# A hybrid encoder block on one core: 27 instead of 24 pairs of the down projection by seven products, activation sums made during up, the value branch without its row norm, taps on ScalarE, weights laid out by the host

## The chip, the cores and the metric

One Trainium2 chip, one of its cores. The time is that of the whole program on the device, in microseconds, as the median of several executions. A second number is the span of one profiled execution, from its first to its last instruction; the profile's rows all come from that execution. TensorE multiplies matrices and writes to PSUM, VectorE and ScalarE do elementwise work on SBUF and PSUM, GpSimd (POOL) does a few tiny operations here, and SyncE (SP) issues nearly all transfers, in order.

## The reference

One layer over 256 tokens of width 2048, in float32. The parts that this change touches are the channel mixer and the way in which every weight is read:

```python
def conv_glu(hn, w_up, conv_w, conv_b, w_down):
    up = hn @ w_up                                   # 2048 -> 2 x 5632
    gate, val = jnp.split(up, 2, axis=-1)
    gate = dwconv_centred(gate, conv_w, conv_b)      # 3 taps along the tokens
    return (jax.nn.gelu(gate, approximate=True) * val) @ w_down

mix = jnp.concatenate([y_ssd, y_pool], axis=-1) @ w_out[i]
h = h + rmsnorm(mix, mix_norm_post[i])
hn = rmsnorm(h, ffn_norm_pre[i])
ff = conv_glu(hn, w_ffn_up[i], ffn_conv_w[i], ffn_conv_b[i], w_ffn_down[i])
h = h + rmsnorm(ff, ffn_norm_post[i])
gate = jax.nn.sigmoid(rmsnorm(h, ple_norm_pre[i]) @ w_ple_gate[i])
h = h + rmsnorm(gate * (p[i] @ w_ple[i]), ple_norm_post[i])
```

In front of it stand an input projection (`w_in`: z, xbc, and dt with u), a state-space mixer and a pooling mixer.

## The kernel before

**Precision.** Each float32 operand is split into a high part (rounded to the form that TensorE takes at full rate) and a low part (the rest). A product of two split operands is three matmuls: high x high, high x low, low x high. `split` makes the parts of a piece of weights: a cast on ScalarE (L152) and a subtraction on VectorE (L153), into one of five pairs of buffers (`whi`, `wlo`). `raw` gives one of three 1 MB buffers that weights are loaded into, on SP's queue through `load` (L119).

**Stages**, in order: dtu (dt and u of the input projection), xbc in three slabs (`feature_major`), z (`token_major`) with the state-space work beside it, wo (the output projection, a `sublayer`), ple's first half, up, down (`dn`, a `sublayer`), ple's second half, the gate (`gt`).

**Up** runs 11 slabs of 512 features. In each, `feature_pairs` makes two pieces `ga` of 256 gate features and two pieces `va` of 256 values, each with tokens along the free side, in two loads of 1 MB; after each load it calls `aside`, which takes the next list of jobs from `work` (88 lists in up). `total` adds the two halves of a piece's PSUM result. The norm in front of up is put on afterwards: `rfb` holds the reciprocal norm of every token along the free side. The gate is multiplied by it (L882), goes through `conv` (centre tap with bias on ScalarE L422, the two others on VectorE L428), through gelu (L884), and is multiplied by `rfb` a second time (L885), which stands for the value's norm; the values are multiplied by that and land in `hid` (L895), six page buffers that stay for down. `rf`, one number per token along the partitions, is what `rfb` was made from.

**Seven products.** Down takes 44 blocks of 128 rows of `w_down`, two at a time: 22 pairs, for each of two halves of the 2048 output columns. An ordinary pair in `token_major` takes 2 blocks x 2 token halves x 2 column halves x 3 = 24 matmuls of 128 x 512. A pair named in `fast` goes through `seven_products`: it takes the pair as a 2 x 2 block product in seven block products instead of eight, 21 matmuls, from four sums of weight blocks (`add_blocks`) and four sums of activation blocks (`pair_sums`); `combine` puts the seven results together at the end of the half. The weight sums of down and of the gate are made during up by `block_sums`, as four jobs: `fetch` the pair, nothing, `add`, `store` to DRAM; the last two in the list are `held` in their page buffers. In down a fast pair then loads three quarters of its weights (`raw`) and its sums (`t`, a page buffer). The activation sums come from `hid_sums`, in a `mid` buffer (three of them): four small operations (L777 to L780) and a split (L781, L782). Those of four pairs (`dn_keep`) are kept in two page buffers from half 0 to half 1. `get_hid` (L903, L904) splits the activations of a pair.

**Around down.** `at` names things to do before a pair of half 1: `back` (before pair 13) loads h again, which was put in DRAM in front of up; `first_gate` (before pair 16) loads the first pair of the gate's weights, casts it twice on ScalarE (L948, L950) and adds into the low part by a transfer on POOL's queue (L949). After each half `sublayer` squares the results on ScalarE (L823) and multiplies them by the norm's gain on VectorE (L824); then h is updated (L831) and transposed for the gate (L380), with ple's second half between.

**Buffers.** 13 page buffers of 1 MB (`page`), three `mid` buffers of half that, PSUM with six `main` and two `misc` banks. The framework orders each engine's instructions before the run, by its own estimate of when each can start; on the chip each engine then runs its own in that order.

Of the kernel before, what the change touches and what calls it, by code (L numbers as in the profile page):

```python
# [16 lines left out]
P = 128  # L17
L = 256
# [33 lines left out]
def build(nc, a, out):  # L52
    x = a["x"][0]
    w_in, w_out, w_up = a["w_in"][0], a["w_out"][0], a["w_ffn_up"][0]
    w_down, w_gate, w_ple = a["w_ffn_down"][0], a["w_ple_gate"][0], a["w_ple"][0]
    out = out[0]

    with tile.TileContext(nc) as tc, \
# [37 lines left out]
        c_dt = DSSD + 1536  # L96
        r0 = wp.tile([P, 2048], F32, tag="raw", bufs=3, name="dtur0")
        for n in range(2):
            first = ins(nc.scalar.dma_start(r0[:, n * 352:(n + 1) * 352],
                                            w_in[:P, c_dt + n * 352:c_dt + (n + 1) * 352]))  # L100
# [55 lines left out]
        def raw(name, src, a_, b_):  # L156
            r = wp.tile([P, 2048], F32, tag="raw", bufs=3, name=name)
            if src is None:
                return r
            last["dma"] = load(r[:, :a_ * b_].rearrange("p (a b) -> p a b", a=a_), src, True)  # L160
            return r
# [46 lines left out]
        def block_sums(name, w, c0, k, held):  # L208
# [4 lines left out]
            def fetch():  # L213
                r = page(f"{name}b{c0}_{k}")
                pg.append(r)
                load(r.rearrange("p (k c) -> p k c", k=2),
                     w[k * P:(k + 2) * P, c0:c0 + 1024].rearrange("(k p) c -> p k c", p=P))
# [6 lines left out]
            def store():  # L224
                if not held:
                    t = dp.tile([P, 2048], F32, tag=f"{name}s{c0}_{k}", bufs=1, name=f"{name}s{c0}_{k}")
                    load(t, pg[0])
                    sums_[name, c0, k] = t, False

            return [fetch], [], [add], [store]  # L230

        def add_blocks(r):

            v = r.rearrange("p (b c) -> p b c", b=4)
            nc.vector.tensor_add(v[:, 0:2], v[:, 0:2], v[:, 1::2])  # L235
            nc.vector.tensor_add(v[:, 3], v[:, 3], v[:, 0])
            nc.vector.tensor_add(v[:, 2], v[:, 2], v[:, 3])

        def seven_products(name, stage, w, k0, c0, a_, acc, alt, start, stop):
# [3 lines left out]
            if (stage, c0, k0) in sums_:  # L243
                r = raw(f"{name}r", None, 0, 0)
                last["dma"] = load(r[:, 512:1536], w[(k0 + 1) * P:(k0 + 2) * P, c0:c0 + 1024], True)
                last["dma"] = load(r[:, :512], w[k0 * P:(k0 + 1) * P, c0:c0 + 512], True)
# [4 lines left out]
                b11 = split(f"{name}a", r[:, :512], 512)  # L251
                b2 = split(f"{name}b", r[:, 512:1536], 1024)
            else:
                r = t = raw(f"{name}r", w[k0 * P:(k0 + 2) * P, c0:c0 + 1024]
                            .rearrange("(k p) c -> p k c", p=P), 2, 1024)
                b11 = split(f"{name}a", r[:, :512], 512)
                b2 = split(f"{name}b", r[:, 1024:], 1024)
# [3 lines left out]
            for x, (wh, wl), c, o, own in (  # L261
                    ("a11", b11, 0, alt[0], True), ("a12", b2, 0, acc[0][0], False), ("s4", b2, 512, acc[0][1], False),
                    ("s1", t13, 0, alt[1], True), ("s3", t13, 512, alt[2], True), ("a22", t42, 0, acc[1][0], False),
                    ("s2", t42, 512, alt[3], True)):
# [26 lines left out]
        def token_major(name, w, c0, ks, get, acc, tail=1, fast=(), alt=None, sums=None, at=()):  # L291
# [3 lines left out]
            for u in range(nu):  # L295
# [3 lines left out]
                if u in fast:  # L299
                    if u == fast[0]:  # L300
# [3 lines left out]
                r = None if f"{name}{k0}_0" in ready else raw(f"{name}r{k0}", w[k0 * P:(k0 + 2) * P, c0:c0 + 1024]  # L304
                                                               .rearrange("(k p) c -> p k c", p=P), 2, 1024)
# [8 lines left out]
                for t, (o, c), (k, wh, wl), q in order:  # L314
                    xh, xl = (v[:, t * P:(t + 1) * P] for v in get(k))
                    xx, ww = ((xh, wh), (xh, wl), (xl, wh))[q]
                    mm(o, xx, ww[:, c:c + o.shape[-1]], k == ks[0] and q == 0, k == ks[-1] and q == 2)
# [3 lines left out]
                aside()  # L321

        def feature_major(name, w, c0, get, acc):

            for u in range(4):
                r = raw(f"{name}r{u}", w[u * 512:(u + 1) * 512, c0:c0 + 512]
                        .rearrange("(k p) c -> p k c", p=P), 4, 512)
# [12 lines left out]
        def feature_pairs(name, w, c0, get, acc):  # L340


            for u in range(2):
                r = raw(f"{name}r{u}", w[u * 1024:(u + 1) * 1024, c0:c0 + 256]
                        .rearrange("(k p) c -> p k c", p=P), 8, 256)
# [97 lines left out]
        for u in range(0, NK, 2):  # L443
            r = [wp.tile([P, 2048], F32, tag="raw", bufs=3, name=f"dtur{u}") if u else r0, page(f"dtur{u + 1}")]
            for j in range(2):
                k = u + j
                if k == 0:
                    last["dma"] = load(r[0][:, 704:1056], w_in[:P, c_dt + 704:c_dt + 1056])
# [3 lines left out]
                for c0, c1 in ((0, 704), (704, 1056)) if k == 1 else ((0, 1056),):  # L452
                    last["dma"] = load(r[j][:, c0:c1], w_in[k * P:(k + 1) * P, c_dt + c0:c_dt + c1])
# [29 lines left out]
        with tc.issue_after(half[0]), tc.issue_after(half[1]):  # L483
# [11 lines left out]
            for a_ in range(4):  # L495
# [17 lines left out]
        load(pmat.rearrange("p (g s t) -> p g s t", g=4, s=2),  # L513
             a["pool_matrix"].rearrange("g (s p) t -> p g s t", p=P))
        poolw = page("poolw")
        load(poolw.rearrange("p (g c d) -> p g c d", g=4, c=2),
             a["pool_w"][0].rearrange("g (c p) d -> p g c d", p=P))
# [122 lines left out]
        def xbc(slab):  # L640
            acc = main(f"xbc{slab}")
            feature_major(f"xb{slab}", w_in, DSSD + slab * 512, hn, acc)
# [88 lines left out]
        token_major("z", w_in, 0, list(range(NK)), hn, zacc)  # L731
# [43 lines left out]

# [144 lines left out]
        def hid_sums(k):  # L920
# [3 lines left out]
            if k not in kept:  # L924
# [6 lines left out]
                if n >= 0:  # L931
                    kept[k] = d
# [157 lines left out]
```

## Time and profile before

| | us |
|---|---|
| median of three runs | 1122.8 (1122.64 to 1123.46) |
| the profiled execution | 1123.46 |
| its span | 1121.6 |

The chain of work that ended last, by what it ran on (share of the span), gives the stages their weight:

```profile
PE va L87 22%; PE ga L87 21%; PE dna L87 14%; PE woa L87 7%; PE xbc L87 6%; PE gt L87 5%; PE z L87 4%; PE dtu L87 4%; PE dns L87 3%; PE dn0s L87 1%; PE dn1s L87 1%; PE ple L87 1%; PE pw L87 1%; PE yd L87 1%; DMA dtur<-w_in 0%
```

`va` and `ga` are up, `dna` the accumulators of down, `dns`, `dn0s` and `dn1s` its four further ones for the seven products. Line 87 is the helper `mm` that issues every matmul, so groups are told apart by tile and not by line. PE is TensorE, PEld its weight loads, DVE VectorE, ACT ScalarE.

Transfers, by queue (packets, megabytes, share of the time of 16 DMA engines), and four of the issues (size, median time from issue to landing):

```profile
q1 hardware_dynamic: 145216, 298.19, 78.8%
q0 software_dynamic: 272, 1.05, 0.5%
...
dnb<-w_ffn_down SPq DMA_DIRECT2D x24, 1024.0 KB, 10.3
dns<-dnb SPq DMA_DIRECT2D x22, 1024.0 KB, 6.9
dn0r<-w_ffn_down SPq DMA_DIRECT2D x10, 1024.0 KB, 6.2
dn1r<-w_ffn_down SPq DMA_DIRECT2D x10, 1024.0 KB, 6.9
```

q1 is SP's queue, q0 POOL's. `dnb` is the fetch of a pair for its weight sums, `dns` their way to DRAM.

### The profile page before, as it was taken

Reading aid. Unit: us, or ns where it says so; the run is one execution under the profiler, and the core shown is the slowest. Engines: PE = TensorE matmul, PEld = TensorE weight load, DVE = VectorE, ACT = ScalarE, POOL = GpSimd, SP = SyncE. Lnnn points to the kernel's source line nnn. Section 1 sums busy time; section 2 is a strip of 40 time slices with the busy share of each in tenths; the row PEclk is TensorE's granted clock in tenths of the full one; section 3 lists DMA queues with packets and bytes.
Section 4 is the critical chain, followed back from the end, with each engine's and each line's share of the span. In section 5 each row is a group of like instructions: output and inputs, shape, how many; then the busy total and the mean of one; then the engine's idle time right before and its main releaser. Section 6 shows DMA issues by size and latency. Waiting matters only on the chain.

```text
span 1121.6 us, 15747 instructions
## 1 busy us (share of the span) xinstructions
PE 1111.2 (99%) x5975; PEld 957.1 (85%) x5975; DVE 928.0 (83%) x1291; ACT 665.4 (59%) x929; POOL 31.1 (3%) x69
## 2 busy tenths in 40 slices
PE   9999999999999999999999999999999999999997
PEld 9999988888888888888888888888888888888876
DVE  6468897799898877877877768878799999899795
ACT  6848663555764554554545545545677777786673
POOL 0200000100100000000000000000000000001001
PEclk9999999999999999999999999999999999999999
DMA  9853447456799989999999898996969688995673
GB/s 361 312 197 104 162 161 277 151 188 189 252 320 349 316 298 340 303 295 313 341 319 310 289 335 303 313 297 218 321 198 336 219 292 295 381 323 175 231 235 107
DMA packets 145996, 300.87 MB, mean 268 GB/s; under 512 B 5504, under 2 KB 98560, under 8 KB 137856
## 3 DMA queue, kind: packets, MB, share of 16 engines
q1 hardware_dynamic: 145216, 298.19, 78.8%
q0 software_dynamic: 272, 1.05, 0.5%
q8 instruction: 47, 0.77, 0.3%
q10 hardware_dynamic: 432, 0.62, 0.2%
q14 instruction: 29, 0.24, 0.1%
HBM read 268.38 MB, written 31.46 MB: 267 GB/s over the span
## 4 chain that ended last, share of the span: by engine, by line
PE 95%; ACT 2%; DVE 1%; issue 1%; DMA 0%; POOL 0%; SPq 0%; POOLq 0%; ACTq 0%
PE va L87 22%; PE ga L87 21%; PE dna L87 14%; PE woa L87 7%; PE xbc L87 6%; PE gt L87 5%; PE z L87 4%; PE dtu L87 4%; PE dns L87 3%; PE dn0s L87 1%; PE dn1s L87 1%; PE ple L87 1%; PE pw L87 1%; PE yd L87 1%; DMA dtur<-w_in 0%
## 5 line engine op out<-in xcount | busy, mean ns | idle before, releaser
L87 PE MATMUL ga<-wox,ug_0h 128*128 128x512 f32 x352 | 125.5, 395 | 0.0
L87 PE MATMUL ga<-wox,ug_1h 128*128 128x512 f32 x352 | 125.1, 394 | 0.0
L87 PE MATMUL va<-wox,uv_1h 128*128 128x512 f32 x352 | 124.8, 393 | 0.0
L87 PE MATMUL va<-wox,uv_0h 128*128 128x512 f32 x352 | 124.8, 393 | 0.0
L87 PE MATMUL ga<-wox,ug_1l 128*128 128x256 f32 x352 | 99.2, 282 | 0.0
L87 PE MATMUL ga<-wox,ug_0l 128*128 128x256 f32 x352 | 99.1, 282 | 0.0
L87 PE MATMUL va<-wox,uv_1l 128*128 128x256 f32 x352 | 99.1, 281 | 0.0
L87 PE MATMUL va<-wox,uv_0l 128*128 128x256 f32 x352 | 99.1, 281 | 0.0
L87 PEld LDWEIGHTS va<-wox,uv_1h 128*128 128x128 f32 x352 | 66.1, 188 | 15.0
L87 PEld LDWEIGHTS va<-wox,uv_0h 128*128 128x128 f32 x352 | 66.1, 188 | 15.0
L87 PEld LDWEIGHTS ga<-wox,ug_0h 128*128 128x128 f32 x352 | 66.1, 188 | 14.9
L87 PEld LDWEIGHTS ga<-wox,ug_1h 128*128 128x128 f32 x352 | 66.1, 188 | 14.9
L87 PEld LDWEIGHTS ga<-wox,ug_0l 128*128 128x128 f32 x352 | 66.2, 188 | 0.1
L87 PEld LDWEIGHTS ga<-wox,ug_1l 128*128 128x128 f32 x352 | 66.2, 188 | 0.0
L87 PEld LDWEIGHTS va<-wox,uv_1l 128*128 128x128 f32 x352 | 66.2, 188 | 0.0
L87 PEld LDWEIGHTS va<-wox,uv_0l 128*128 128x128 f32 x352 | 66.2, 188 | 0.0
L87 PE MATMUL dna<-dn_0h,hs 128*128 128x512 f32 x160 | 50.1, 393 | 0.0
L87 PE MATMUL dna<-dn_1h,hs 128*128 128x512 f32 x160 | 49.9, 393 | 0.0
L235 DVE TENSOR_TENSOR dnb<-dnb 128x1024 f32<-128x1024 f32 x24 | 29.3, 1222 | 14.0 <-DMA dnb<-w_ffn_down 14.0
L903 ACT CAST hs<-hid 128x512 fp32r<-128x512 f32 x44 | 27.1, 617 | 18.3 <-PE dna L87 18.3
L904 DVE TENSOR_TENSOR hs<-hid,hs 128x512 fp32r<-128x512 f32 x44 | 30.2, 686 | 9.1 <-ACT hs L903 9.0
L428 DVE SCALAR_TENSOR_TENSOR fc<-gr,vt,fc 128x255 f32<-128x255 f32 x88 | 36.8, 479 | 0.1
(1909 smaller groups left out, 3060.3 us busy)
## 6 DMA issues: line engine op xcount, KB each, us to landing
dnb<-w_ffn_down SPq DMA_DIRECT2D x24, 1024.0 KB, 10.3
dns<-dnb SPq DMA_DIRECT2D x22, 1024.0 KB, 6.9
dn0r<-w_ffn_down SPq DMA_DIRECT2D x10, 1024.0 KB, 6.2
dn1r<-w_ffn_down SPq DMA_DIRECT2D x10, 1024.0 KB, 6.9
zr<-w_in SPq DMA_DIRECT2D x8, 1024.0 KB, 5.2
dtur<-w_in SPq DMA_DIRECT2D x14, 528.0 KB, 8.5
wo0r<-w_out SPq DMA_DIRECT2D x7, 1024.0 KB, 5.5
wo1r<-w_out SPq DMA_DIRECT2D x6, 1024.0 KB, 5.7
```

The costliest lines, as they stand in the source:

```text
L87: last["pe"] = ins(nc.tensor.matmul(o, lhsT, rhs, start=start, stop=stop, skip_group_check=True))
L235: nc.vector.tensor_add(v[:, 0:2], v[:, 0:2], v[:, 1::2])
L428: nc.vector.scalar_tensor_tensor(o[:, lo:hi], i[:, lo + d:hi + d], vec(wcol + j * wstep + f), o[:, lo:hi], op0=ALU.mult, op1=ALU.add)
L903: nc.scalar.copy(t[:, :512], src)
L904: nc.vector.tensor_sub(t[:, 512:], src, t[:, :512].bitcast(F32))
```

## The change

1. **More fast pairs.** Half 0 of down takes 14 of its 22 pairs by seven products and half 1 takes 13, for 12 and 12. `block_sums` makes 27 + 4 sets of sums for 24 + 4, at 14/5 slots of `work` apart instead of 3; the two held ones have no fourth slot.
2. **Activation sums from up.** For eight pairs (`dn_stored`, fast in both halves) the sums of activations are made during up, in an `hs` buffer, and stored to DRAM; in down `hid_sums` loads them on POOL's queue into a `mid` buffer, in both halves. For the other fast pairs they are made in down, in each half. The kept page buffers go.
3. **Values without the norm.** The second multiplication by `rfb` goes. The token's factor is put on in `sublayer` instead (`row=rf`): as a scale of the squares and in a three-operand multiply with the gain.
4. **Taps on ScalarE.** `conv` of up is written out per half slab: three taps on ScalarE into `cv`, `tp` and the source itself, added by two VectorE adds over two features at once; gelu per half slab.
5. **Weights in tiles by the host.** Every weight comes as tiles of 128 rows x 2048 (1056 for dtu), in the order in which they are read, so that one load reads one stretch of memory. In `pairs` the first block of a pair has its column halves swapped, so that the three quarters that a fast pair needs lie together: one load in place of two. The pooling constants are laid out the same way.
6. **Order.** `add_blocks` takes four instructions of 512 columns for one of 1024 and two of 512. The seven products come in another order, with the split of the second half of the sums first. `first_gate` (now `first`) stands before pair 15 instead of 16, `back` behind the last pair instead of before pair 13.

```diff
             def store():
-                if not held:
-                    t = dp.tile([P, 2048], F32, tag=f"{name}s{c0}_{k}", bufs=1, name=f"{name}s{c0}_{k}")
...
-            return [fetch], [], [add], [store]
+            return [[fetch], [], [add]] + [[store]] * (not held)
 
         def add_blocks(r):
             v = r.rearrange("p (b c) -> p b c", b=4)
-            nc.vector.tensor_add(v[:, 0:2], v[:, 0:2], v[:, 1::2])
-            nc.vector.tensor_add(v[:, 3], v[:, 3], v[:, 0])
-            nc.vector.tensor_add(v[:, 2], v[:, 2], v[:, 3])
+            for i, j in ((1, 0), (0, 3), (3, 1), (2, 3)):
+                nc.vector.tensor_add(v[:, i], v[:, i], v[:, j])
...
             if (stage, c0, k0) in sums_:
-                r = raw(f"{name}r", None, 0, 0)
-                last["dma"] = load(r[:, 512:1536], w[(k0 + 1) * P:(k0 + 2) * P, c0:c0 + 1024], True)
-                last["dma"] = load(r[:, :512], w[k0 * P:(k0 + 1) * P, c0:c0 + 512], True)
+                r = raw(f"{name}r")
+                last["dma"] = load(r[:, 512:], w[c0 // 1024, k0 // 2][:, 512:], True)
...
-            t13 = split(f"{name}c", t[:, :1024], 1024)
             t42 = split(f"{name}d", t[:, 1024:], 1024)
+            t31 = split(f"{name}c", t[:, :1024], 1024)
...
-                        nc.scalar.activation(junk, b, AF.Square, accum_out=q)
-                        nc.vector.tensor_mul(mg[t][:, c], b, gain[:, c])
+                        if row:
+                            nc.scalar.activation(junk, b, AF.Square, scale=row[t], accum_out=q)
+                            nc.vector.scalar_tensor_tensor(mg[t][:, c], b, row[t], gain[:, c], op0=ALU.mult, op1=ALU.mult)
...
-        dn_fast, gt_fast, dn_keep = ((2, 3, 5, 7, 8, 10, 12, 13, 15, 16, 18, 19), (2, 3, 5, 7, 8, 10, 12, 13, 15, 16, 18, 19)), ((4, 6), (1, 2)), (3, 8, 13, 18)
+        dn_fast, gt_fast = ((2, 3, 4, 5, 7, 8, 9, 11, 12, 13, 15, 16, 18, 19), (2, 3, 5, 7, 8, 9, 11, 12, 13, 15, 16, 18, 19)), ((4, 6), (1, 2))
+
+        dn_stored = (2, 3, 5, 8, 11, 13, 16, 19)
...
-                work[3 * i + 2 + j].extend(jobs)
+                work[14 * i // 5 + 1 + j].extend(jobs)
...
+        def hid_sums_jobs(k):
+            o = []
+            def make():
+                o.append(lp.tile([P, 1024], F32R, tag="hs", bufs=2, name=f"he{k}"))
+                hid_sums_of(k, o[0][:, 512:].bitcast(F32), o[0])
+            def store():
+                kept[k] = dp.tile([P, 1024], F32, tag=f"hsum{k}", bufs=1, name=f"hsum{k}")
+                load(kept[k], o[0].bitcast(F32))
+            return [make], [store]
+        for u in dn_stored:
+            for j, jobs in enumerate(hid_sums_jobs(2 * u)):
+                work[u // 2 * 8 + u % 2 * 2 + 6 + j].extend(jobs)
...
-            cv = conv(f"fc{s}", sc, 3, V_FCW + 4 * s, NF, V_FCB + 4 * s)
-            nc.scalar.activation(cv, cv, AF.Gelu_apprx_tanh)
-            nc.vector.tensor_tensor(cv.rearrange("p (f t) -> p f t", f=4), cv.rearrange("p (f t) -> p f t", f=4),
-                                    rfb.unsqueeze(1).to_broadcast([P, 4, L]), op=ALU.mult)
+                c, l = (m[:, i * 512:(i + 1) * 512].rearrange("p (f t) -> p f t", f=2) for m in (cv, tp))
+                for f in range(2):
+                    w = V_FCW + 4 * s + 2 * i + f
+                    nc.scalar.activation(c[:, f], v[:, f], AF.Identity, bias=vec(V_FCB + 4 * s + 2 * i + f), scale=vec(w + NF))
+                    nc.scalar.activation(l[:, f], v[:, f], AF.Copy, scale=vec(w))
+                    nc.scalar.activation(v[:, f], v[:, f], AF.Copy, scale=vec(w + 2 * NF))
+                nc.vector.tensor_add(c[:, :, 1:], c[:, :, 1:], l[:, :, :L - 1])
+                nc.vector.tensor_add(c[:, :, :L - 1], c[:, :, :L - 1], v[:, :, 1:])
+                g = cv[:, i * 512:(i + 1) * 512]
+                nc.scalar.activation(g, g, AF.Gelu_apprx_tanh)
...
+            o = mid(f"hd{k}", F32R)
+            if k in kept:
+                nc.gpsimd.dma_start(o.bitcast(F32), kept[k])
+                d = sums_in(o)
             else:
-                d = kept[k]
+                d = hid_sums_of(k, sp.tile([P, 512], F32, tag="junk", bufs=1, name=f"hs{k}"), o)
...
-                      fast=dn_fast, sums=hid_sums, at={13: back, 16: first_gate})
+                      fast=dn_fast, sums=hid_sums, at={15: first, NF // 2: back}, row=rf)
...
+    def tiles(w, nk, nc):
+        k, c = w.shape
+        return w.reshape(k // P // nk, nk, P, c // nc, nc).transpose(3, 0, 2, 1, 4).reshape(c // nc, k // P // nk, P, nk * nc)
+    def pairs(w):
+        r = tiles(w, 2, 1024)
+        return np.concatenate([r[..., 512:1024], r[..., :512], r[..., 1024:]], axis=-1)
```

More of the change, by code (lines that the diff above doesn't have):

```diff
@@ L154, in split, with raw @@
             return hi, lo
-        def raw(name, src, a_, b_):
+        def raw(name, src=None):
             r = wp.tile([P, 2048], F32, tag="raw", bufs=3, name=name)
-            if src is None:
-                return r
-            last["dma"] = load(r[:, :a_ * b_].rearrange("p (a b) -> p a b", a=a_), src, True)
+            if src is not None:
+                last["dma"] = load(r, src, True)
             return r
@@ L447, in build @@
                 if k == 0:
-                    last["dma"] = load(r[0][:, 704:1056], w_in[:P, c_dt + 704:c_dt + 1056])
+                    last["dma"] = load(r[0][:, 704:1056], w_dtu[0][:, 704:1056])
                     xload(1, 2)
@@ L804, in __call__, with sublayer @@
                             a22=(h2[:, P:], l2[:, P:]))
-        def sublayer(name, w, ks, get, gain, h, vnext, panel=Panel, fast=((), ()), sums=None, at=()):
+        def sublayer(name, w, ks, get, gain, h, vnext, panel=Panel, fast=((), ()), sums=None, at=(), row=None):
             mg = [page(f"{name}m{t}") for t in range(2)]
```

116 lines of the change are left out of this document (59 added, 57 removed).

## The prediction

> **What bounds the kernel now.** I read the page first: its busy line, its chain, its costliest groups.
>
> ```profile
> span 1121.6 us, 15747 instructions
> ...
> PE 1111.2 (99%) x5975; PEld 957.1 (85%) x5975; DVE 928.0 (83%) x1291; ACT 665.4 (59%) x929; POOL 31.1 (3%) x69
> ...
> PE 95%; ACT 2%; DVE 1%; issue 1%; DMA 0%; POOL 0%; SPq 0%; POOLq 0%; ACTq 0%
> ...
> L235 DVE TENSOR_TENSOR dnb<-dnb 128x1024 f32<-128x1024 f32 x24 | 29.3, 1222 | 14.0 <-DMA dnb<-w_ffn_down 14.0
> ...
> L428 DVE SCALAR_TENSOR_TENSOR fc<-gr,vt,fc 128x255 f32<-128x255 f32 x88 | 36.8, 479 | 0.1
> ```
>
> TensorE is 95% of the chain that ends last; VectorE and DMA are 1% and 0%. Work taken from another engine is worth nothing here unless TensorE waited for it. So I cut the span at up (314 to 789) and at the two halves of down, and added a stretch in which only x was loaded, in rows of 8 KB:
>
> ```profile
> core 0: us, PE busy (x) PEld busy (x) DVE busy (x) ACT busy (x) POOL busy (x), PEclk, DMA share, GB/s
> 32.60:37.30 4.70, 4.70 (x31) 4.70 (x30) 2.11 (x3) 2.90 (x3) 0.24 (x1) 1.00 1.01 417
> 314.00:789.00 475.00, 475.00 (x2724) 416.93 (x2724) 383.71 (x498) 239.06 (x315) 0.00 (x0) 1.00 0.94 308
> 789.00:903.00 114.00, 114.00 (x496) 92.64 (x496) 105.59 (x147) 82.17 (x109) 0.00 (x0) 1.00 0.76 259
> 903.00:1017.00 114.00, 113.95 (x494) 92.29 (x493) 104.97 (x143) 84.39 (x109) 3.35 (x8) 1.00 0.92 325
> ```
>
> TensorE is busy throughout all three stages at full clock, with VectorE at 81%, 93% and 92% beside it. Busy need not mean fast, so the rate comes from the chain in order of time (start, length, what, matmuls): an ordinary pair, then one by seven products.
>
> ```profile
> 949.13 5.56 PE dna L87 x24
> 954.69 0.69 PE dns L87 x3
> 955.38 1.40 PE dna L87 x6
> 956.78 0.69 PE dns L87 x3
> 957.47 0.69 PE dn1s L87 x3
> 958.16 0.69 PE dna L87 x3
> 958.85 0.70 PE dn1s L87 x3
> 959.55 5.55 PE dna L87 x24
> ```
>
> Twenty-four matmuls take 5.55 us, 0.231 each; the 21 of seven products take 4.86. A half of 12 fast and 10 ordinary pairs should then take 12 x 4.86 + 10 x 5.55 = 113.8 us, and the two of them 227.6; the first down matmul starts at 788.9 and ple's first at 1016.7, 227.8 later. Down has one wait to give back, at pair 16 of half 1; ScalarE's timeline there, then who waited for that pair's weight sums:
>
> ```profile
> 980.37 1.89 ACT L950 CAST gtfh<-gtf 128x2048 fp32r<-128x2048 f32 x1
> ...
> 985.72 1.04 ACT L152 CAST dn132ch<-dn132t 128x1024 fp32r<-128x1024 f32 x1
> ...
>   PEld dna L87: 0.5, 1
> ```
>
> The sums were issued at 976.7 and landed 6.5 us later; ScalarE had spent 978.6 to 982.3 on the first gate pair (1.91 + 1.89 us), then caught up with five casts, and came to them at 985.7. Two matmuls start 0.45 us apart where 0.23 is usual: 0.22 us lost.
>
> **The sum: TensorE.** Fast pairs go from 12 + 12 to 14 + 13. Three pairs x 3 matmuls x 0.231 = **-2.08 us**. Everything else computes the same matmuls.
>
> **That wait.** `first` moves a pair earlier, so that ScalarE's 3.8 us fall before pairs 14 and 15 instead of 15 and 16, and weight sums may be fetched sooner: of 13 page buffers hid had 6, mg 2, pl 1 and the kept activation sums 2; without the kept ones four are left for weight sums instead of two. I take the 0.22 us as gone: **-0.2** (bounds 0 and -0.22).
>
> **Up, VectorE.** Removed: 88 taps x 0.479 = 36.8 us; values by rfb, 11 x 1.225 = 13.5. Added: 44 adds of 2 x 255, at most the 0.69 of a 128x512 add: 30.4. Block sums become four instructions of 0.69 (2.76) for 1.22 + 2 x 0.69 (2.60), 31 of them for 28: +12.8. Activation sums for eight pairs, each four of 0.29 and one of 0.685: 14.7. Net +7.6, 391 of 475 us (82% for 81%). **ScalarE:** 88 more taps, at most the 0.594 of the centre tap: +52; casts and halved gelus +7; 298 of 475 (63% for 50%). Neither ends a wait of TensorE now and neither is full, so I take **0**; the cover is the five buffers of split weights, each 16 matmuls or 2.8 us long, 11 us at best. Six taps in a row (3.6 us) plus a gelu fit into it. If it were gone, each of 22 half-slabs could cost up to a tap, 0.6 us: +13 at the other end, which I leave far out because now whole slabs (4 taps and a 1.06 us gelu) pass without a wait. gr, fc and the new ft take all three mid buffers, but gr and ft are free before the value part ends, and ft is not written until the next gate's first 11.2 us are over.
>
> **Down, VectorE.** A computed activation sum is 1.84 us, a fast pair splits 0.69 + 3 x 1.22 = 4.35 against 2.44 for an ordinary one. Half 0: six sums fewer, two fast pairs more, 105.6 - 11.0 + 3.8 = 98 of 112.6 us; half 1: three fewer, one more, 105.0 - 5.5 + 1.9 = 101 of 113.3. Both easier than before: 0.
>
> **DMA.** An ordinary pair loads 1.05 MB, a fast one 0.79 plus 1.05 of weight sums, a stored activation sum adds 0.52. Half 1 before: 10 x 1.05 + 12 x 1.84 + 4.2 for h and the first gate pair = 36.7 MB in 114 us, 322 GB/s (the row says 325). After: 9 x 1.05 + 13 x 1.84 + 8 x 0.52 + 4.2 = 41.7 MB in 113.3 us, **368 GB/s**; half 0 comes to 321. The host's tiles make rows 6 to 8 KB long, and such rows ran at 417; at the old mix, 325 / 0.92 gives 353. I take the first (nearest: same row length), 88% busy, and cost 0; the other end is the first rival. In up the rows of w_up grow from 1 KB to 8 KB, so up should fall below its share of 0.94 in spite of some 10 MB more; it is hidden either way.
>
> **Moved.** `back` goes behind the last pair. Its two loads now queue on SP behind the last weights (issued 991 to 994 before) and take 9.7 us to land, so about 1004; the first use is at 1018.7: 0, and about 1 us for each us past that. `first` moves one pair earlier: one load on SP, one adding load on POOL behind ScalarE's 1.9 us; POOL then holds the sums of pairs 16 and 19 behind it (second rival). The row factor makes four Squares and four multiplies longer, 0.742 for 0.69; at the end of half 1 ple's 24 matmuls lie beside it, and the first transpose (1020.2) came while 2.6 us of them were left. 0, or +0.3 if not.
>
> Sum: -2.08 - 0.2 = -2.3. The profiled execution took 1123.46 us, 1.9 more than its span; so 1121.2, and as the runs' median lies 0.66 lower, **1120.5**.
>
> **Rivals.**
>
> *DMA becomes the bound in half 1 (slower).* It decides if the engines carry less than 368 GB/s there. At 353: 41.7 MB take 118.1 us, 4.8 over TensorE's 113.3; less 2.3 gained, **1125.3**. For: share 0.92 now, and 0.5 MB more per stored pair from a second queue. Against: long rows at 417, and three raw buffers and four page buffers to run ahead. 0.14. The Trainium skill speaks for it: "DMA: Bandwidth & Descriptors", section Specifications, gives about 358 GB/s as one core's share of HBM; by that, 41.7 MB would take 116.5 us and the run 1123.7. The 417 of the x rows disagrees here, where one core runs alone.
>
> *Stored sums land late on POOL's queue.* A sum can be fetched when the third fast pair before it has let go of its mid buffer. With two fast pairs between (pair 5 of half 0, pair 13 of both) that is 9.7 us plus three products, 11.8. The nearest rows: 6.5 us (weight sums, 1 MB on SP) to 14.4 (the adding 1 MB load on POOL, plus 1.4 to issue). At the upper end 4 us late, three or four times: +12 to 16; in the middle +6, **1126.5**. Against: half a megabyte, no adding. 0.08.
>
> *Small waits eat it.* Pairs 7, 8, 9 in a row cost VectorE 6.9 + 5.0 + 6.9 = 18.8 us against 14.6 of TensorE, 4.2 behind, where two computed in a row were 4.0 behind before. A slip of 0.2 to 1 us in each half: **1122**. 0.16.
>
> *More comes back.* The gate's second half lost 0.6 us waiting for one split (gt112bl), the front 3; layout and the new order of the seven products touch both: **1119.4**. 0.12.
>
> **How the numbers follow.** Forecast 0.50 (1119.8 to 1121.2), rivals 0.14, 0.08, 0.16, 0.12. A change of 0.2%, 2.25 us, is about what a measurement here tells from none; it puts the line at 1120.55, just above the forecast, so I split that 0.50 into 0.30 below it and 0.20 above. Faster 0.30 + 0.12 = 0.42; same 0.20 + 0.16 = 0.36; slower 0.14 + 0.08 = 0.22. Range 1119.0 to 1125.6: from the further gain to DMA at 353, leaving out POOL and the tails. The likeliest's own range is 1119.8 to 1121.2.
>
> **What would show it.** Right: down lasts 225.7 us from its first matmul to ple's, at 0.231 a matmul, with no wait of TensorE in its chain; up still 475 us, VectorE about 82% and ScalarE 63% of it; DMA in half 1 near 368 GB/s at a share near 0.9. Wrong: a share near 1 in half 1 with TensorE waiting for casts of weight sums (first rival); TensorE waiting for a product of stored sums while POOL's loads take over 11 us (second); TensorE waiting in up on splits behind taps; the transposes after down waiting for h.

## The result, and the profile after

The changed kernel takes **1127.69 us** in the median of five runs (1127.41 to 1128.98), the kernel before 1122.8; the ratio of the runs is 1.0047, 95% interval 1.0035 to 1.0058. It is slower by about half a per cent. The profiled execution took 1127.69, with a span of 1125.8, 4.2 more than before. The page, its busy line and its chain of waits:

```profile
span 1125.8 us, 15797 instructions
...
PE 1112.4 (99%) x5966; PEld 955.3 (85%) x5966; DVE 919.1 (82%) x1280; ACT 703.6 (62%) x1033; POOL 39.9 (4%) x85
...
PE 89%; DVE 4%; ACT 4%; DMA 1%; issue 1%; POOL 0%; POOLq 0%; ACTq 0%; DVEq 0%
```

TensorE's share of the chain fell from 95% to 89%, and VectorE and ScalarE have 4% each: it now waits for them now and then. Up, half 0 and half 1 of down as windows (columns as before: length, busy time of PE, PEld, DVE, ACT and POOL with instructions, granted clock, DMA share, GB/s):

```profile
314.00:793.00 479.00, 476.31 (x2717) 415.41 (x2716) 379.56 (x513) 274.19 (x419) 1.34 (x2) 1.00 0.86 329
793.00:906.00 113.00, 113.00 (x493) 91.92 (x492) 102.42 (x131) 85.04 (x108) 4.84 (x9) 1.00 0.84 314
906.00:1019.90 113.90, 112.92 (x490) 91.54 (x489) 102.08 (x129) 83.83 (x106) 5.42 (x11) 1.00 0.93 354
```

Up was busy 475.00 of 475.00 before; now TensorE stands still for 2.7 us of it, with VectorE at 79% and ScalarE at 57%, so no engine is full. From the first matmul of a stage to that of the next (us; up from the first `va` to the first `dna`, down to the last `dna`, then ple and the gate to the last `gts`, the gate's last product, then the rest):

| | up | down | ple, gate | rest | span |
|---|---|---|---|---|---|
| before | 469.04 | 227.55 | 95.81 | 9.30 | 1121.6 |
| after | 474.16 | 225.95 | 96.88 | 9.44 | 1125.8 |

In front of `va` the kernel gained 0.5, but that is scatter: in the runs below that start like the changed kernel, the first `va` comes anywhere from 319.16 to 319.98 us. So the 4.2 us are -0.5 + 5.1 - 1.6 + 1.1 + 0.1. What was to be gained in down came, mostly; up lost more. Whom TensorE waits for in up and down of the changed kernel, and did not before (total us, times, longest; in the gate 0.4 us for `gt_1l` is new as well):

```profile
PE va L88 <- DVE uv_0l L152: 1.3, 2, 0.8
PE ga L88 <- DVE ug_0l L152: 1.1, 2, 0.5
PE dna L88 <- DVE hs L935: 1.0, 1, 1.0
```

`uv_0l` and `ug_0l` are low parts of split weights of up. Matmul by matmul, up has seven places (at 404, 416, 451, 496, 642, 720 and 732 us) where one starts 0.28 to 0.92 us late, with smaller losses right around them: 18 late starts that make 4.9 of the 5.1 us. The chain of waits into the first of them, in order of time (start, length, what):

```profile
398.63 0.70 DVE gr L907
...
399.36 0.60 ACT fc L912
...
401.25 0.40 ACT ft L913
401.65 0.95 ACT ug_0h L151
...
402.62 1.24 DVE ug_0l L152
...
403.90 0.39 PE ga L88
```

This is to be read backwards: the matmul waits for the low part, that for the cast on ScalarE (L151), and the cast for five taps in front of it (the first and the last are shown), which wait for a gate half slab that TensorE has just finished. The weights had landed at 398.9. In the kernel before, the casts of the next weights stand ahead of the taps (here at 398.18 and 400.96, the first tap at 401.92).

### The profile page after: what moved, and what is told of

Its sections match the earlier page's. It is cut to its first block, busy times and chain, and to the rows that moved or that the text cites. A ratio compares the mean times of both kernels' runs of the same rounds, so it can differ in the third digit from the quotient of the medians.

```text
span 1125.8 us, 15797 instructions
## 1 busy us (share of the span) xinstructions
PE 1112.4 (99%) x5966; PEld 955.3 (85%) x5966; DVE 919.1 (82%) x1280; ACT 703.6 (62%) x1033; POOL 39.9 (4%) x85
## 3 DMA queue, kind: packets, MB, share of 16 engines
q0 software_dynamic: 2448, 9.44, 2.5%
## 4 chain that ended last, share of the span: by engine, by line
PE 89%; DVE 4%; ACT 4%; DMA 1%; issue 1%; POOL 0%; POOLq 0%; ACTq 0%; DVEq 0%
PE va L88 20%; PE ga L88 19%; PE dna L88 12%; PE woa L88 7%; PE xbc L88 6%; PE gt L88 5%; PE dtu L88 4%; PE z L88 4%; PE dns L88 3%; PE dn0s L88 2%; DMA dn1r<-w_down 1%; PE dn1s L88 1%; PE ple L88 1%; PE pw L88 1%; PE yd L88 1%
## 5 line engine op out<-in xcount | busy, mean ns | idle before, releaser
L232 DVE TENSOR_TENSOR dnb<-dnb 128x512 f32<-128x512 f32 x108 | 74.1, 687 | 1.9 <-DMA dnb<-w_down 0.2
L352 ACT COPY hid<-va 128x256 f32<-128x256 f32 x44 | 16.0, 373 | 60.9 <-PE va L88 60.9
L352 ACT COPY gr<-ga 128x256 f32<-128x256 f32 x44 | 15.9, 376 | 53.6 <-PE ga L88 53.6
L88 PE MATMUL dna<-dn_0h,hs 128*128 128x512 f32 x136 | 42.9, 394 | 1.0 <-DVE hs L935 1.0
L88 PE MATMUL dna<-dn_1h,hs 128*128 128x512 f32 x136 | 43.0, 393 | 0.0
L912 ACT ACTIVATE fc<-gr,vt 128x256 f32<-128x256 f32 x44 | 26.2, 595 | 25.6 <-DVE gr L907 25.6
```

The costliest lines, as they stand in the source:

```text
L88: last["pe"] = ins(nc.tensor.matmul(o, lhsT, rhs, start=start, stop=stop, skip_group_check=True))
L232: nc.vector.tensor_add(v[:, i], v[:, i], v[:, j])
L352: nc.scalar.copy(o[:, f * L:(f + 1) * L], acc[f][:, L:])
L912: nc.scalar.activation(c[:, f], v[:, f], AF.Identity, bias=vec(V_FCB + 4 * s + 2 * i + f), scale=vec(w + NF))
```

## The experiments

Each place of loss had several candidates. For up: (A) ScalarE's added taps; (B) the stores of activation sums on SP's queue, which wait there for VectorE with weight loads queued behind them; (C) VectorE too full. For down's remaining waits at pairs 15 to 17: (D) a burst of transfers, the gate's adding load among them; (E) the load of half 1 as a whole. Theory F came later. The kernel before took 1123.04 to 1123.11 us in the jobs of the experiments; ratios are to it.

**1. The outer taps back on VectorE**, still by half slab; no `ft`.

```diff
-                    nc.scalar.activation(l[:, f], v[:, f], AF.Copy, scale=vec(w))
-                    nc.scalar.activation(v[:, f], v[:, f], AF.Copy, scale=vec(w + 2 * NF))
-                nc.vector.tensor_add(c[:, :, 1:], c[:, :, 1:], l[:, :, :L - 1])
-                nc.vector.tensor_add(c[:, :, :L - 1], c[:, :, :L - 1], v[:, :, 1:])
+                    nc.vector.scalar_tensor_tensor(c[:, f, 1:], v[:, f, :L - 1], vec(w), c[:, f, 1:], op0=ALU.mult, op1=ALU.add)
+                    nc.vector.scalar_tensor_tensor(c[:, f, :L - 1], v[:, f, 1:], vec(w + 2 * NF), c[:, f, :L - 1], op0=ALU.mult, op1=ALU.add)
```

> The changed kernel with its outer taps back on VectorE (two multiply-adds per feature, still per half slab; ft and its mid buffer go); all else as changed. Theory A (in up ScalarE's fixed order puts the cast of the next weights behind five or six taps that wait for VectorE's gr, which waits for the end of a gate piece, so TensorE starves at seven places): the seven waits go, up (first va of slab 0 to first down matmul) falls from 474.2 us back to about 469.5, total 1122.5 to 1123. Theory B (SP's queue: weight loads stand behind the stores of activation sums): the waits stay, total 1126 to 1128. Theory C (VectorE is too full with 31 block sums of four instructions and eight activation sums): the taps add 7 us to VectorE, so it gets slower, 1128 or more.

Measured: 1127.18, ratio 1.0038 (1.0023 to 1.0052), up 472.98. Three quarters of the loss stay without the added work on ScalarE. The trace has the same order on a smaller scale: at 490.71 two centre taps stand ahead of the cast of `ug_0h` (491.71), whose weights had landed at 484.47, and on VectorE four outer taps stand ahead of the subtraction for it (494.13). TensorE then starts 0.91 us late at 495.40.

**2. No stored sums**: all activation sums are made in down, in each half.

```diff
-        dn_stored = (2, 3, 5, 8, 11, 13, 16, 19)
+        dn_stored = ()
```

> The changed kernel with no activation sums made in up (dn_stored empty): all are made in down, in both halves; no stores and no loads of them. Theory A: up keeps its seven waits (about +5 us against before), and down, where VectorE has 8 x 1.84 us more in each half, gets near 114 us a half and loses 1 to 4 us: 1128 to 1131. Theory B: up's waits go, so 1123 to 1126 by what down loses. Theory C: most of up's waits go as well.

Measured: 1126.02, 1.0025 (1.0016 to 1.0035). Up is 469.04, as before the change, to the hundredth; down is 230.03, for there VectorE and ScalarE now come late with sums and splits. So up's loss comes with the stored sums, and down needs them.

**3. The kernel before with the taps on ScalarE**, and nothing else: part 4 of the change alone.

```diff
-            cv = conv(f"fc{s}", sc, 3, V_FCW + 4 * s, NF, V_FCB + 4 * s)
-            nc.scalar.activation(cv, cv, AF.Gelu_apprx_tanh)
+                    nc.scalar.activation(c[:, f], v[:, f], AF.Identity, bias=vec(V_FCB + 4 * s + 2 * i + f), scale=vec(w + NF))
+                    nc.scalar.activation(l[:, f], v[:, f], AF.Copy, scale=vec(w))
+                    nc.scalar.activation(v[:, f], v[:, f], AF.Copy, scale=vec(w + 2 * NF))
...
```

> The kernel before with one thing of the change alone: three taps on ScalarE per half slab, two adds on VectorE, gelu per half slab (the second multiplication by rfb stays, per half slab). Theory A: waits like those of the changed kernel appear in up, 1125 to 1128. Theory B: there are no stores of activation sums, so 1122.8 plus or minus 1. Theory C: VectorE has 6 us less to do, 1122.8 or a little under.

Measured: 1123.1, 0.9999 (0.999 to 1.0008), up 469.04. The taps by themselves cost nothing: A and C fall in their plain form.

**4. The eight stores on POOL's queue**, else the changed kernel.

```diff
-                load(kept[k], o[0].bitcast(F32))
+                nc.gpsimd.dma_start(kept[k], o[0].bitcast(F32))
```

> The changed kernel with the eight stores of activation sums issued on POOL's queue instead of SP's, so that no weight load stands behind them. Theory A: no change, 1127 to 1128.5. Theory B: the waits of up go, 1122.5 to 1123.5.

Measured: 1123.73, 1.0007 (0.9997 to 1.0017), up 469.04, down 227.13, ple and gate 96.94. The same bytes go to the same place by another queue, and up's whole loss is gone. This looked like B; it took four more runs to see that it isn't.

**5. The gate's first pair at pair 10, 6. without the adding load, 7. h back at pair 13, 8. twelve and twelve fast pairs** (2, 3, 5, 7, 8, 10, 11, 13, 15, 16, 18 and 19 in both halves) all start from run 4 and are about down.

```diff
# 5 (part of a line)
...at={15: first, NF // 2: back}...   before
...at={10: first, NF // 2: back}...   this run
# 6
-            nc.scalar.activation(lo, r, AF.Copy, scale=-1.0)
-            nc.gpsimd.dma_start(lo, w_gate[0, 0], accum_op=ALU.add)
             nc.scalar.copy(hi, r)
+            for j in range(2):
+                nc.vector.tensor_sub(lo[:, j * 1024:(j + 1) * 1024], r[:, j * 1024:(j + 1) * 1024], hi[:, j * 1024:(j + 1) * 1024].bitcast(F32))
# 7 (part of a line)
...at={13: back, 15: first}...   this run
```

> The version with the stores of activation sums on POOL's queue (1123.7), and the gate's first pair fetched before pair 10 of half 1 instead of 15. Theory D (what is left is DMA in half 1: between 972 and 1000 the gate pair's two loads, stored sums and weights come together at a share of 1.0, and the weights of pair 17 and the sums of pair 16 land 12 to 14 us after issue): the two waits of down (1.0 and 1.2 us) get smaller or go, since pairs 9 to 11 lie among ordinary ones; down from its first matmul to the gate's last falls from 321.2 to about 319.5, total 1122 to 1123. Theory E (the total load of half 1, not the burst, is too much): the waits only move, 1123.5 plus or minus 0.5.

Measured: 1123.28, 1.0012 (1.0 to 1.0024); down 227.47, its waits now at pairs 11 and 12; ple and gate 95.79. The waits moved with the gate's loads and did not shrink (2.6 us of late starts in down, 2.4 in run 4), which D had not expected.

> The same base, the gate's first pair still before pair 15, its low part made by VectorE (two subtractions of 1.22 us) instead of a second load that adds on POOL's queue: 1 MB less to move in half 1. Theory D: the waits of pairs 16 and 17 go, total 1121.8 to 1122.8. Theory E: waits half as long, 1123. If VectorE is what is short in down, the two subtractions cost up to 2.4 us: 1125.

Measured: **1120.22, 0.9975 (0.9964 to 0.9985)**, faster than both kernels; down 224.74 without a wait, ple and gate 95.79. E falls: without a wait, half 1 still moves 353 GB/s at a share of 0.91. The runs lie within 1.1 us; those of run 5 spread from 1122.67 to 1128.41.

> The same base, h loaded again before pair 13 as in the kernel before, instead of behind the last pair. Theory D: 2 MB more in the burst of half 1, its waits grow by 1 to 4 us: 1124.5 to 1127. If instead h came too late at the end (the gate's waits of 0.2 and 0.5 us), those go and it gets 0.7 us faster.

Measured: 1123.85, 1.001 (1.0 to 1.0019); down 227.51, ple and gate 97.22. Nothing comes back by moving h.

> The same base with 12 and 12 fast pairs (2, 3, 5, 7, 8, 10, 11, 13, 15, 16, 18, 19), eight of them with stored sums: three pairs go back to 24 matmuls. The TensorE term alone: +2.08 us, 1125.8. If the waits of down come from DMA and VectorE being short around the added pairs, these 2.2 us go and the two cancel: 1123.5 to 1124.

Measured: 1123.63, 1.0006 (0.9996 to 1.0015); down 227.29. Here three pairs fewer change nothing, for the waits cover them; run 12 asks again without the waits.

**9. The changed kernel with run 6's edit alone, 10. the kernel before with it.** The diff is that of run 6.

> The changed kernel, its eight stores of activation sums on SP's queue as they were, and only the gate's first pair split by VectorE (ScalarE copies the high part, two subtractions make the low part; no transfer on POOL adds into it). If the two causes are separate, this takes off what the same edit took off with the stores on POOL (1123.73 - 1120.22 = 3.5) and leaves up at 474.1: 1124.2, down near 223.2 to 225 without a wait on split weights, the gate near 95.8. If the adding transfer were only harmful because of where up ends and how the queue then stands, up stays 474 and down does not change: 1127.7.

Measured: 1125.24, 1.0018 (1.0009 to 1.0027); up 474.07, down 224.74, ple and gate 95.76. The causes in up and in down are separate; this edit takes off 2.5 here and 3.5 above.

> The kernel before with only the gate's first pair split by VectorE instead of by a transfer on POOL that adds. If that transfer hurts by itself, this takes off the 0.2 to 1 us of waits that down of before has at pairs 16 and 17: 1122.2 to 1122.8 (0.999 to 0.9997). If it hurts only where the queues of half 1 are as full as the three more pairs and the loads of stored sums make them, before does not move: 1123.1, ratio 1.000. If the whole gain of 1120.22 came from this edit and none from the pairs: 1119.6 or so (0.997).

Measured: 1122.9, 0.9997 (0.9987 to 1.0006). In the kernel before, the adding load and the copy cost nothing: even the 0.22 us at pair 16 are still there. That they hurt in the changed kernel because its half 1 is fuller is likely, and not shown.

**11. The stores one slot later, still on SP.**

```diff
-            return [make], [store]
+            return [make], [], [store]
```

> The changed kernel with one edit: the store of each activation sum stands one slot of the list of jobs later, still on SP's queue (one slot is one load of 1 MB or 5.3 us of up). If it is SP's wait for the sums that blocks the weight loads behind it (up to 12.3 us of one wait, against some 11 to 16 us that the buffers hold), 5.3 us less of each wait leave the loads in time mostly: up 469 to 471, 1123 to 1125. If the stores cost by their transfers or by being eight more issues on SP, wherever they stand, up stays 474 and the time 1127.7.

Measured: 1128.53, 1.0045 (1.003 to 1.006), up 474.14. It decided nothing: the framework, which draws up SP's order by its own estimate, left the stores where they were (at 379.8, 391.9, 440.2 us and so on, within 0.3 of the changed kernel).

**12. Run 6 with twelve and twelve fast pairs** (the list of run 8).

> The best version so far (stores on POOL, no adding transfer) with 12 and 12 fast pairs in place of 14 and 13. Here no wait covers the pairs, so the three pairs show their price alone. Nine matmuls of 0.231: 2.1 us more in down, 226.8 for 224.74, and 1122.3 in all (about 0.9992). If the pairs were worth nothing on TensorE (their products slowed by the split of the sums): 1120.2. If the transfers of half 1 still cost, fewer fast pairs would load more bytes per pair and the difference would be above 2.1: 1123 and over.

Measured: 1122.42, 0.9993 (0.9983 to 1.0002); down 226.74 for 224.74. Three pairs are worth 2.00 us of down and 2.2 in all.

**13. The stores six slots later**, some 32 us, which does move them behind two to four weight loads in SP's order.

```diff
-            return [make], [store]
+            return [make], [], [], [], [], [], [], [store]
```

> The changed kernel with the store of each activation sum six slots of the list of jobs later (some 32 us of up), still on SP's queue. One slot later left SP's order of transfers as it was, so that run was the changed kernel again; six slots do move the stores behind two to four loads of weights. If SP's wait for sums that are not yet made is the cause, the sums are long there when the store's turn comes, no load waits behind it, up is 469.04 and the time near that with the stores on POOL: 1123.7, and SP waits for sums some 27 us in up in place of 73. If eight more stores on SP cost wherever they stand (issue time or transfers), up stays near 474 and the time near 1127.7.

Measured: 1127.16, 1.0035 (1.0023 to 1.0048), up 472.39. B falls: SP no longer waits for finished sums, and two thirds of the loss are still there. ScalarE's timeline of this run (start, length, what, idle time before) shows why:

```profile
442.24 0.72 ACT L352 COPY gr<-ga 128x256 f32<-128x256 f32 x2 [5.52 <-PE ga L88]
444.65 0.61 ACT L912 ACTIVATE fc<-gr,vt 128x256 f32<-128x256 f32 x1 [1.69 <-DVE gr L907]
...
446.45 0.49 ACT L913 ACTIVATE ft<-gr,vt 128x256 f32<-128x256 f32 x1
446.86 1.03 ACT L151 CAST ug_0h<-ug31r 128x1024 fp32r<-128x1024 f32 x1
```

The weights of that cast had landed at 437.25, 9.6 us before, while ScalarE stood idle for 5.5 and 1.7 us. It could not take the cast: in its order five taps are ahead of it, and they wait for the gate. The Trainium skill, "PSUM — Partial Sum Buffer", section "Engine vs sequencer instructions", says that ScalarE's and VectorE's queues are strictly first in, first out; the trace agrees. The same stretch with the stores on POOL (run 4):

```profile
442.82 1.05 ACT L151 CAST ug_0h<-ug31r 128x1024 fp32r<-128x1024 f32 x1
...
444.04 1.06 ACT L151 CAST ug_1h<-ug31r 128x1024 fp32r<-128x1024 f32 x1
...
447.23 0.60 ACT L912 ACTIVATE fc<-gr,vt 128x256 f32<-128x256 f32 x1 [0.24 <-DVE gr L907]
```

Same instructions, casts first. Hence theory F: what costs is that order; and it comes about because the framework takes the weights to come later when SP has the stores too, and so lets the taps, which it thinks ready earlier, go ahead. It is the order that A spoke of, brought about by the stores that B spoke of.

**14. Casts ahead of taps, stores on SP where they were; 15. the same with the stores six slots later.** The taps become a job of a later slot, issued behind the last cast:

```diff
+                def conv_half(s=s, i=i, sc=sc, cv=cv, tp=tp, v=v):
+                    with tc.issue_after(last["act"]):
...
+                work[1].insert(0, conv_half)
```

> The changed kernel, stores on SP and where they were, with one thing forced: the taps of a half slab stand behind the casts of the next piece's second load on ScalarE (the job that issues them is called one load later, and each of its ScalarE instructions is told to be issued behind the last cast). The run six slots later has up at 472.39, and at 448 us a cast of weights that had landed 9.6 us before stands behind five taps. Theory F: the stores only made the framework expect the weights later and put taps ahead of casts, and that order is what costs; then up falls to 469.0 to 470.5 although SP still waits 72 us for sums, and the time to 1122.7 to 1124.5. Theory B: the loads that stand behind the stores land too late whatever ScalarE's order; then up stays at 472.5 to 474.

Measured: 1124.32, 1.0009 (1.0 to 1.0019); up **469.36**, and the view of waits lists none of TensorE's in it. What SP waited for in up, in the changed kernel and then in this run:

```profile
SPq L118 <- DVE he L774: 72.6, 8, 12.3
```

```profile
SPq L118 <- DVE he L774: 69.3, 8, 11.9
```

SP stands as long as ever for the eight sums (`he`), up to 11.9 us at a time, with weight loads behind them. At the place shown above the load lands at 446.01, 8.8 us later than in run 13, ScalarE casts it at 446.09, and TensorE loses 0.1 us, for 0.9 at this place in the changed kernel. B is refuted, and of F it is shown what costs: late loads still had room, the taps ahead of the casts took it. (The moved job takes VectorE's adds along; but in the chain of the first section the subtraction starts 0.02 us behind the cast, so that wait was ScalarE's.) Why the framework chose the order stays a guess of F; no run asks it.

> Both edits: the stores six slots later on SP, and the casts ahead of the taps on ScalarE. Theory F, and theory B as well as a half of it: nothing is late on SP and no tap stands in front of a cast, so up is 469.04 and the time 1122.7 to 1124.5. If up is still above 471 here, eight more transfers on SP cost by themselves, by the time that their issue or their bytes take.

Measured: 1124.17, 1.0008 (0.9999 to 1.0017), up 469.14.

**16. Run 6 with a second, plain load of the same megabyte on POOL; 17. run 6 with ScalarE's scaled copy put back**, to take run 6's edit apart (lines against run 6).

```diff
# 16
+            nc.gpsimd.dma_start(r, w_gate[0, 0])
# 17
+            nc.scalar.activation(lo, r, AF.Copy, scale=-1.0)
             nc.scalar.copy(hi, r)
```

> The version without the adding transfer (1120.22), plus one plain load on POOL of the same megabyte into the buffer that SP has just loaded (the same values again). If it is the bytes of the second load that stretch half 1 (41.7 MB again), this gives back most of the 3.5 us: 1122.5 to 1124, with waits at pairs 15 to 17. If it is the adding (a transfer that reads its target as well, 15.0 us to land), a plain one costs a part: 1120.2 to 1121.5, with landings of weight sums at 8 to 11 us and not 12 to 15.

Measured: 1124.84, 1.0021 (1.0011 to 1.003); down 228.83, with 1.96 us lost at pair 15, whose weight sums landed at 980.63. This looks as if the megabyte were enough, but the trace does not say so. In its chain of waits (start, length, what):

```profile
972.04 8.59 DMA dn130t<-dns
```

The sums of pair 15 took 8.6 us, no longer than in run 6 (9.0), and the plain megabyte landed in 7.2 us. But SP issued the sums at 972.04, behind another load that waited for its buffer; in run 6 they went at 966.57, ahead of that load. ScalarE also stood for 1.9 us before the gate's cast, which here waits for the second load. So this run loses by an order again, and whether the adding load costs by its bytes or by its adding stays open.

> The version without the adding transfer, plus ScalarE's scaled copy of the gate's first pair (1.9 us), which that version had lost with the transfer; its result is overwritten by VectorE's two subtractions. If the gain came from the transfer, this stays at 1120.2 to 1120.5. If it came from ScalarE's 1.9 us at pairs 15 to 17, 1122 to 1124 with waits behind casts and no long landings.

Measured: 1121.46, 0.9985 (0.9975 to 0.9994); down 224.74 as in run 6, ple and gate 96.94 for 95.79. Around pairs 15 to 17 SP's loads stand in the order of run 4, so the transfer is what this run lacks against it: of run 6's 3.5 us, 2.4 are the adding transfer, in down, and 1.1 ScalarE's copy, in the gate.

## Why the prediction was wrong, step by step

**What bounds the kernel, and three pairs at -2.08: right.** Down without its waits measured 2.00 us between 12 + 12 and 14 + 13 pairs (runs 12 and 6). In the changed kernel itself -1.6 is left, because one wait stayed.

**Up at 0: this is the step that failed, by 5.1 us** of the 7.2 between forecast and result. (The others: the gate 1.1, down 0.7, the rest 0.1, less 0.5 in front of `va`; 0.7 because the profiled execution before lay that much above its median, and the one after on it.) It asked whether the added work fits: engines not full, five split buffers of 11 us as cover, six taps and a gelu shorter than that. All of that is true (79% and 57% busy; run 3: the taps cost nothing), though one product in it is not: 88 x 0.479 is 42.2, and 36.8 is the row's busy time, in which overlapping instructions count once. It took the order on ScalarE as given and the cover with it. But the buffers cover the taps only if the casts stand ahead of them; with the taps ahead, the cast of the next weights hangs on the end of the previous piece, and the whole way of the chain above (add, multiply, five taps, cast, subtraction, from 397.8 to 403.9) has to pass while TensorE works off one load of 5.6 us. What turned the order round is an item whose place the working left out: eight stores on SP's queue in up. I counted the VectorE operations of the moved activation sums, and their bytes in the "some 10 MB more" that I called hidden, but not where they stand on the queue. Either half alone costs nothing: taps without stores (run 3, up 469.04), stores without taps ahead (run 14, 469.36). The other end of that step's range, 13, did hold the loss; I gave it no weight because whole slabs of taps passed before without a wait.

**The wait at pair 16, -0.2: replaced.** It went; what had made it is open, for run 10, without the copy and the adding load, still has it. One of 1.15 us came at pair 17, whose weights took 12.6 us to land. In the chain of waits of the changed kernel:

```profile
977.44 12.63 DMA dn1r<-w_down
...
990.17 1.06 ACT dn_0h L151
```

Without the adding load (run 6) that landing takes 8.5 us, and down is 2.8 us shorter than before: the 2.08, the 0.33 of its waits, 0.23 for a matmul of ple that stood in it before, and 0.2 that was not followed.

**DMA in half 1 at 0, from 417 GB/s: wrong by 1.2 us in the changed kernel (run 9), by 2.4 with the stores on POOL (run 17), and the rival's 353 at a full share wrong too.** The half moved 354 GB/s at a share of 0.93, that is 381 when full: enough for the 368 that the half as a whole was to need. (The 321 given for half 0 does not come out of its terms, 38.3 MB in 112.6 us or 340; it measured 314.) Where it broke is a short stretch. The first gate pair comes twice there, and while its second, adding load is under way (974.4 to 989.4), full engines carry less. The changed kernel, and then run 6 in the same part of half 1:

```profile
978.00:982.00 4.00, 4.00 (x19) 3.28 (x18) 3.49 (x5) 4.00 (x6) 0.00 (x0) 1.00 1.01 345
982.00:986.00 4.00, 4.00 (x19) 3.23 (x19) 4.00 (x5) 3.40 (x6) 0.00 (x0) 1.00 1.07 285
...
994.00:1000.00 6.00, 5.73 (x25) 4.71 (x26) 5.08 (x7) 2.98 (x5) 0.00 (x0) 1.00 1.02 425
```

```profile
980.00:984.00 4.00, 4.00 (x19) 3.28 (x18) 4.00 (x6) 3.86 (x5) 1.18 (x2) 1.00 0.96 390
```

With the adding load 345 and 285 GB/s at shares of 1, after it 425; without it 390 at 0.96. That this rate is what made the weights of pair 17 late fits run 17, but no run changes the rate alone. A mean over 114 us could not show that; the 14.4 us that the same load took to land before could have.

**Down's VectorE at 0: right**, with the sizes 102.4 and 102.1 us for 98 and 101; no wait of the changed kernel comes from it (the one at pair 17 ends with VectorE's `hs`, which starts late because the weights do). **Stored sums on POOL (second rival): did not happen**; the five issued in half 1 land in 5.4 to 9.1 us, the slowest of all in 10.6, and TensorE waits for none. **`back` at 0: right**, though later than said: h landed at 1008.9 and 1011.4, not 1004.

**The gate at 0, or +0.3: it was +1.1.** Run 17 shows that ScalarE's scaled copy brings it (96.94 with it, 95.79 without, the transfer gone in both), and run 5 that it is gone when that work is done earlier. With the copy, casts of the gate's weights and the copies of the transposes stand in another order on ScalarE, and in run 17 a matmul at 1027.5 starts 0.48 us late; the rest of the 1.1 was not followed to its end.

**The forecast** of 1120.5 is what the change gives with two edits: 1120.22 with the stores off SP and the adding load replaced. That the number comes so close is partly luck: run 6 lies 2.9 us under the kernel before in its own job, where the sum had 2.3. The three pairs were there as counted; what the forecast missed is one order, one transfer and one copy. It had named the sign for it, "TensorE waiting in up on splits behind taps", but no rival carried it.

## What to carry to other kernels

When a change moves work, list its transfers with it, queue by queue, and ask not only whether there is time but in which order each engine will do it: an in-order engine that has work of a later need ahead of work of an earlier one loses with half its time idle. Where a framework draws up that order from an estimate, one more transfer can turn it round at a distant place; so compare the order of the instructions before and after, and pin what must come first. A cure that works (another queue) does not yet name the cause: only putting the order right with the transfers left alone did. And an experiment's own edit can turn an order: run 16 added one load and got another queue.

## What the runs showed of the hardware

**The same transfers on another queue.** From 320 to 788 us up's transfers run at 330 to 334 GB/s at a share of 0.86 or 0.87 with the stores on SP (the changed kernel, runs 13 and 14) or on POOL (run 4). The Trainium skill, "DMA: Bandwidth & Descriptors", section "Issuing engines are not separate DMA queues", says that another issuing engine saves only the time of issuing; the transfers agree. The 5.1 us that came back in run 4 are no exception: run 14 has 4.8 of them with the stores on SP.

**A short wait, then half the clock.** In run 16 TensorE stood for 1.79 us at pair 15, then for 0.22, and a moment later its granted clock was down:

```profile
983.00:987.00 4.00, 4.00 (x12) 3.17 (x13) 4.00 (x6) 3.17 (x4) 0.00 (x0) 0.60 0.87 347
```

From 983 to 986 it is 0.50, with matmuls 0.43 us apart in place of 0.23; so 2.0 us in which TensorE stood still came to 4.1 us of down (228.83 for the 224.74 of run 6). The late starts of 0.92 and 1.15 us in the changed kernel left the clock at 1.00. A wait of 1.89 us near the end of the program went both ways: in the changed kernel the clock is 0.50 right behind it, in the kernel before it stays at 1.00 for 3 us more. The Trainium skill, "TensorE: Matmul & The Clock Gate", section "What's actually happening", puts the window of idleness that drops the clock at about 3.4 us; here 1.79 us, with 0.22 more behind them, went before a drop.
